# Seven block products in place of eight for one column chunk of gate and up, with a lag of four turns and nine pairs

## The chip, the cores and the metric

The kernel runs on one core of one Trainium2 chip. The metric is the time of one execution in microseconds of the device; several executions are timed and the median is given.

## The reference

The input is 256 tokens of 1024 float32 numbers. Four layers follow each other, and each has three blocks: a feed-forward block (FFN), a mixer, a second FFN. An FFN adds half of a SwiGLU to the tokens, with d_ff = 2816:

```
y = x * rsqrt(mean(x*x) + 1e-6) * g
x = x + 0.5 * ((silu(y @ w_gate) * (y @ w_up)) @ w_down)     # 1024 -> 2816 -> 1024
```

The mixers are, by layer: a gated short convolution, multi-head latent attention (MLA), a spatial gating MLP, and the convolution again. Each starts with the same norm and adds its result to x. All is float32.

## The kernel before

**Tiles and streams.** The 256 tokens are two tiles of 128 tokens. Each tile has a stream, a generator that walks through all twelve blocks (`stream`, `ffn`, `conv`, `mla`, `spatial`); each `yield` ends a turn. The loop at the end of `program` calls `advance` for tile 1 and then for tile 0 in each round, and tile 0 has had LAG = 3 turns ahead of that. So every engine gets its instructions in an order written out by hand, and all five engines run in that order. `later(n, fn)` puts a step off by n calls of `advance`.

**Products.** Each float32 operand is split in two parts, high and low, that TensorE takes in its fp32r format, and each product is three matmuls: high by high, high by low, low by high (`products`, L317, L318, L320). A weight unit is 1024 numbers per partition. `Weights` loads a unit into a raw buffer (N_RAW = 6), ScalarE makes the high part (L107), VectorE the low part (L113), as a pair of tiles in a pool of N_UNITS = 8 pairs. A unit is made AHEAD = 4 units before the leading tile needs it and is used by both tiles, by tile 1 three turns after tile 0. A turn of a tile in gate, up or down is one unit: six matmuls of 512 columns.

**An FFN.** The 2816 columns of gate and up are cut in FF_CHUNKS: five chunks of 512 columns and one of 256. For each chunk, eight k-tiles of 128 rows are accumulated in a bank of PSUM for gate (`gate_done` takes the bank through Silu on ScalarE, L475) and for up (`up_done` multiplies it by the gate on VectorE, L483, and turns 32 by 32 blocks over, L485). The first three of these run in a group (`linear_group`), then the rest one after the other (`linear`). The product is written to DRAM and read back transposed (`Turned`), split again by `take` (L308, L309) and multiplied by down (`rows_into_x`); there, the last DOWN_TAIL = 12 of the 22 k-tiles are done for the left half of the columns first and then for the right half.

**Between blocks.** `residual` adds each half of the result to x (L401, L403). `prepare_x` then squares it (L384), turns it over, by TensorE (`turn_by_pe`, L283, L444) or by VectorE and DRAM (L418, L424, L428, L434), multiplies by the gain and splits it (L275, L276) into `lhs[t][h]`. The norm's factor is applied later, with the evictions from PSUM. `normed` idles two turns of the stream, during which the other tile's matmuls run.

**Memory.** Most small tiles come from one pool of N_SLOTS = 34 slots of 2 KB per partition.

Of the kernel before, what the change touches and what calls it, by code (L numbers as in the profile page):

```python
# [40 lines left out]
N_UNITS = 8  # L41
N_RAW = 6
N_SLOTS = 34
# [4 lines left out]
LAG = 3  # L48
H_READ, H_TAKE = 7, 2
DOWN_TAIL, OUT_TAIL = 12, 4  # L50
# [86 lines left out]
@with_exitstack  # L137
def trunk(ctx: ExitStack, tc: tile.TileContext, x, positions, norm_g, ffn_gate, ffn_up, ffn_down,
          conv_w_in, conv_k, conv_w_out, mla_w_a, mla_q_norm, mla_w_uq, mla_kv_norm, mla_w_ukv,
          mla_q_gain, mla_k_gain, mla_w_o, sg_w_in, sg_v_norm, sg_w_s, sg_b, sg_w_out, out):  # L140
    const = ctx.enter_context(tc.tile_pool(name="const", bufs=1))
    raw_pool = ctx.enter_context(tc.tile_pool(name="raw", bufs=N_RAW))
    w_pool = ctx.enter_context(tc.tile_pool(name="w", bufs=N_UNITS))
# [5 lines left out]
    pools = const, raw_pool, w_pool, slots, bigs, small, dram, banks  # L149
    ins = (x, positions, norm_g, ffn_gate, ffn_up, ffn_down, conv_w_in, conv_k, conv_w_out, mla_w_a, mla_q_norm, mla_w_uq,  # L150
           mla_kv_norm, mla_w_ukv, mla_q_gain, mla_k_gain, mla_w_o, sg_w_in, sg_v_norm, sg_w_s, sg_b, sg_w_out, out)
    order = program(Blank(), [Blank()] * len(pools), None, *ins)
    with tc.manual_schedule(engines=MANUAL):
        program(tc.nc, pools, order, *ins)


def program(nc, pools, order, x, positions, norm_g, ffn_gate, ffn_up, ffn_down,
            conv_w_in, conv_k, conv_w_out, mla_w_a, mla_q_norm, mla_w_uq, mla_kv_norm, mla_w_ukv,
            mla_q_gain, mla_k_gain, mla_w_o, sg_w_in, sg_v_norm, sg_w_s, sg_b, sg_w_out, out):
    const, raw_pool, w_pool, slots, bigs, small, dram, banks = pools  # L160
# [32 lines left out]
    def run_due():  # L193
# [6 lines left out]
    W = Weights(nc, raw_pool, w_pool, {  # L200
        "gate": ffn_gate, "up": ffn_up, "down": ffn_down, "conv_in": conv_w_in, "conv_out": conv_w_out, "w_a": mla_w_a,
        "w_ukv": mla_w_ukv, "w_uq": mla_w_uq, "w_o": mla_w_o, "sg_in": sg_w_in, "sg_out": sg_w_out}, order)
    in_chain = [False] * NT
    pause = [0] * NT
    own = [0] * NT
# [12 lines left out]
    neg_half = fixed([P, 4], "neg_half")  # L218
    causal_r = fixed([P, P], "causal_r", F32R)
# [13 lines left out]
    def start():  # L233
        half = D // 2
        nc.sync.dma_start(out=xs[0][:, :half], in_=x[0, :P, :half])
        nc.scalar.dma_start(out=rows[0][: n_rows[0]], in_=norm_g.rearrange("i j (k p) -> (i j k) p", p=P))
        nc.sync.dma_start(out=xs[0][:, half:], in_=x[0, :P, half:])
# [5 lines left out]
        nc.gpsimd.memset(neg_half, -0.5)  # L243
        nc.vector.tensor_copy(out=ident_r, in_=ident)
# [24 lines left out]
        later(41, lambda: nc.vector.tensor_copy(out=causal_r, in_=causal))  # L269
# [21 lines left out]
    class Turned:  # L291
# [53 lines left out]
    def rows_into_x(t, a, m, n_kt, tail, factor, then):  # L345
# [33 lines left out]
    sums_of_x = [[None, None] for _ in range(NT)]  # L379

# [9 lines left out]
    def factor(sums):  # L390
        total = tiny(1, "total")
        nc.gpsimd.tensor_tensor(out=total, in0=sums[0], in1=sums[1], op=ALU.add)  # L392
        return power(total, EPS, 1.0 / D, 1, "rstd")
# [15 lines left out]
    def prepare_x(t, h, i, which, halves_by_dma):  # L409

        g = gain_at(i, which, h)
        lhs[t][h] = None
        later(1, lambda: square_x(t, h))
        if not halves_by_dma[h]:
            later(X_TURN, lambda: turn_by_pe(t, h, g))
            return
        z = slot([P, 4, 4, 32])
        nc.vector.transpose(z.rearrange("p j k b -> p k j b"), x_half(t, h).rearrange("p (k j b) -> p k j b", j=4, b=32))  # L418
# [12 lines left out]
        def take():  # L431
            xg = slot([P, 4, P])
            for k in range(4):
                nc.scalar.activation(xg[:, k, :].rearrange("p (i b) -> p i b", b=32), y[:, :, k], AF.Copy, scale=g[:, k : k + 1])  # L434
            lhs[t][h] = split(xg, [P, 4, P])

        later(X_WRITE, write)
        later(X_READ, read)
        later(X_TAKE, take)

    def turn_by_pe(t, h, g):
        tr = transposed([xs[t][:, (4 * h + k) * P : (4 * h + k + 1) * P] for k in range(4)])
        xg = slot([P, 4, P])
        nc.vector.tensor_tensor(out=xg, in0=tr, op=ALU.mult, in1=g.unsqueeze(2).broadcast_to([P, 4, P]))  # L444
        lhs[t][h] = split(xg, [P, 4, P])
# [11 lines left out]
    def normed(t, idle):  # L457
# [3 lines left out]
        return Lhs(t), factor(sums_of_x[t])  # L461


    def ffn(t, i, j, _, then):
        a, r = yield from normed(t, IDLE_FIRST if i + j == 0 else (IDLE_DMA, IDLE_PE)[j])
        gate, up, down = (("gate", i, j), ("up", i, j), ("down", i, j))
        hs = [None] * len(FF_CHUNKS)
        sg = [None] * len(FF_CHUNKS)
        z = []
        recs = []  # L470
# [6 lines left out]
        def up_done(n, ps):  # L477
            w = FF_CHUNKS[n][1]
            nk = sum(w for _, w in FF_CHUNKS[n - n % 2 : n - n % 2 + 2]) // P
            if n % 2 == 0:  # L480
                z[:] = [big([P, 4, nk, 32]), 0]
# [6 lines left out]
            if z[1] == nk:  # L488
                recs.append(Turned(z[0], nk))

        def body():
            yield from linear_group(t, a, [(gate, 0, lambda ps: gate_done(0, ps)), (up, 0, lambda ps: up_done(0, ps)),
                                           (gate, 512, lambda ps: gate_done(1, ps))], 512, NK)
            for n, (c, w) in enumerate(FF_CHUNKS):
# [3 lines left out]
                if n > 0:  # L498
                    up_done(n, (yield from linear(t, a, up, c, w, NK)))
                    yield  # L500
            yield from rows_into_x(t, lambda k: hs[k // 4], down, DFF // P, DOWN_TAIL, 0.5, then)

        def take(n):
            hs[n] = recs[n // 2].take(n % 2 * 4)

        events = {}
        for n in range(len(FF_CHUNKS)):
            k = 4 * n
            at = DFF // 64 + (k if k < DFF // P - DOWN_TAIL else DFF // P - DOWN_TAIL + (k - DFF // P + DOWN_TAIL) // 2)
            if n % 2 == 0:  # L510
                events.setdefault(at - H_READ, []).append(lambda n=n: recs[n // 2].read())
            events.setdefault(at - H_TAKE, []).append(lambda n=n: take(n))
        for at, _ in enumerate(body()):
            for event in events.get(at, ()):
                event()
            yield


    def conv(t, i, ia, shared, then):
# [49 lines left out]
        yield from rows_into_x(t, lambda k: ms[k // 4], ("conv_out", ia), NK, OUT_TAIL, 1.0, then)  # L569
# [27 lines left out]
    def spatial(t, i, ic, _, then):  # L597
# [3 lines left out]
        def v_done(v):  # L601
# [5 lines left out]
            if len(vs) == 2:  # L607
                rv.append(factor(sums))
# [41 lines left out]
        yield from rows_into_x(t, lambda k: ms[k // 4], ("sg_out", ic), NK, OUT_TAIL, 1.0, then)  # L650
# [129 lines left out]
    def mla(t, i, ib, shared, then):  # L780
# [174 lines left out]
        yield from rows_into_x(t, lambda k: os_[k // 4], ("w_o", ib), NK, OUT_TAIL, 1.0, then)  # L955
# [11 lines left out]
    def stream(t):  # L967
        for h in range(2):
            yield
            turn_by_pe(t, h, gain_at(0, 0, h))  # L970
            later(1, lambda h=h: square_x(t, h))
        for n, (kind, i, j) in enumerate(blocks):
# [17 lines left out]
    def advance(t):  # L990
# [3 lines left out]
        run_due()  # L994

# [35 lines left out]
```

## Time and profile before

| | |
|---|---|
| median of 3 runs | 1873.46 us (1873.39 to 1873.93) |
| the profiled execution's own time | 1871.69 us |
| its span, from the first to the last instruction | 1870.0 us |
| mean granted clock of TensorE, as a share of full speed | 0.996 |
| DMA, mean over the span | 214 GB/s |

Everything below is read from one profiled execution. Engines: PE is TensorE's matmuls, PEld its weight loads, DVE VectorE, ACT ScalarE, POOL GpSimd, SP the engine that issues most DMAs. Matmuls overlap in the array, so the time between the starts of two matmuls, and not the duration of one, tells how fast they go.

### The profile page before, as it was taken

What the parts mean: (1) busy time and instruction counts of PE and PEld (TensorE: products, weight loads), DVE (VectorE), ACT (ScalarE), POOL (GpSimd) and SP (SyncE); (2) the same over time, 40 slices, a digit from 0 to 9 for tenths busy, and PEclk for the clock granted to TensorE, in tenths of its full rate; (3) what the DMA queues carried; (4) which work ended last, traced back from release to release, by engine and by line L of the source; (5) the groups of instructions that cost most, each with busy time, mean ns of one, the idle gap of its engine ahead of it and who ended that gap; (6) DMA issues with size and microseconds to landing.
All of it is one profiled execution on the core that took longest, in us unless ns stands there. A gap on an engine that the chain in (4) does not pass through costs nothing.

```text
span 1870.0 us, 23382 instructions
## 1 busy us (share of the span) xinstructions
PE 1838.4 (98%) x8518; PEld 1508.3 (81%) x8518; DVE 1122.9 (60%) x1357; ACT 919.8 (49%) x1300; POOL 95.8 (5%) x222
## 2 busy tenths in 40 slices
PE   8999999999999989999999999999999999999999
PEld 6888877888888868788888888788888888778887
DVE  6556676555656576655565565655656565675563
ACT  5344545344544476544454456453445455545352
POOL 1000000000501031000010000000000000000000
PEclk9999999999999998999999999999999999999999
DMA  7678656678767740667876787566877686656683
GB/s 260 217 236 238 216 180 207 215 241 233 233 216 245 226 141 13 203 218 228 251 246 215 227 248 229 161 220 213 258 218 241 216 263 193 216 181 213 216 257 112
DMA packets 228981, 400.26 MB, mean 214 GB/s; under 512 B 17127, under 2 KB 77697, under 8 KB 228865
## 3 DMA queue, kind: packets, MB, share of 16 engines
q1 hardware_dynamic: 227856, 397.08, 67.5%
q8 instruction: 66, 1.08, 0.2%
q0 software_dynamic: 608, 1.11, 0.2%
q10 hardware_dynamic: 400, 0.57, 0.1%
q14 instruction: 51, 0.41, 0.1%
HBM read 365.67 MB, written 33.03 MB: 213 GB/s over the span
## 4 chain that ended last, share of the span: by engine, by line
PE 94%; DVE 3%; ACT 2%; issue 1%; DMA 0%; POOL 0%; DVEq 0%; ACTq 0%
PE acc L317 31%; PE acc L320 30%; PE acc L318 30%; PE tr L283 1%; DVE wlo L113 1%; PE acc L908 1%; PE acc L935 1%; DVE s L537 1%; ACT whi L107 0%; DVE x L401 0%; DVE s L535 0%; ACT s L833 0%; ACT s L275 0%; PE acc L624 0%; DMA s<-in_norm_g_dram 0%
## 5 line engine op out<-in xcount | busy, mean ns | idle before, releaser
L317 PE MATMUL acc<-whi,s 128*128 128x512 f32 (+1 forms) x2664 | 1025.3, 385 | 3.8 <-ACT s L275 2.9
L318 PE MATMUL acc<-wlo,s 128*128 128x512 f32 (+1 forms) x2664 | 1020.3, 383 | 1.5 <-DVE wlo L113 1.5
L320 PE MATMUL acc<-whi,s 128*128 128x512 f32 (+1 forms) x2664 | 989.1, 383 | 0.0
L113 DVE TENSOR_TENSOR wlo<-raw,whi 128x1024 fp32r<-128x1024 f32 (+1 forms) x634 | 749.0, 1212 | 282.7 <-ACT whi L107 277.9
L107 ACT ACTIVATE whi<-raw 128x1024 fp32r<-128x1024 f32 (+1 forms) x634 | 640.9, 1049 | 185.3 <-PE acc L320 155.8
L317 PEld LDWEIGHTS acc<-whi,s 128*128 128x128 f32 x2664 | 500.8, 188 | 108.7 <-ACT s L275 4.3
L320 PEld LDWEIGHTS acc<-whi,s 128*128 128x128 f32 x2664 | 500.9, 188 | 106.7 <-DVE s L276 1.0
L318 PEld LDWEIGHTS acc<-wlo,s 128*128 128x128 f32 x2664 | 501.1, 188 | 105.7 <-DVE wlo L113 2.3
L475 ACT ACTIVATE s<-acc,rstd 128x512 f32<-128x512 f32 (+1 forms) x96 | 62.6, 652 | 403.9 <-PE acc L320 403.9
L483 DVE SCALAR_TENSOR_TENSOR s<-acc,rstd,s 128x512 f32<-128x512 f32 (+1 forms) x96 | 67.8, 707 | 152.7 <-PE acc L320 152.7
L384 ACT ACTIVATE s<-x 128x512 bf16<-128x512 f32 x48 | 30.2, 630 | 160.3 <-DVE x L403 115.2
L309 DVE TENSOR_TENSOR s<-big,s 128x512 fp32r<-128x512 f32 x96 | 61.2, 638 | 50.4 <-ACT s L308 48.4
L392 POOL TENSOR_TENSOR total<-ss,ss 128x1 f32<-128x1 f32 x26 | 14.1, 544 | 1469.5 <-ACT s L384 1469.5
L403 DVE SCALAR_TENSOR_TENSOR x<-acc,x 128x512 f32<-128x512 f32 x32 | 22.1, 690 | 104.1 <-PE acc L320 104.1
L276 DVE TENSOR_TENSOR s<-s,s 128x512 fp32r<-128x512 f32 (+1 forms) x58 | 39.9, 688 | 73.1 <-ACT s L275 73.1
L485 DVE STREAM_TRANSPOSE big<-s 128x512 f32<-128x512 f32 (+1 forms) x96 | 64.1, 667 | 3.3
L308 ACT ACTIVATE s<-big 128x512 fp32r<-128x512 f32 x96 | 54.7, 582 | 16.5 <-DMA big<-turn 16.5
L275 ACT ACTIVATE s<-s 128x512 fp32r<-128x512 f32 (+1 forms) x58 | 36.5, 629 | 50.6 <-DVE s L544 28.6
L434 ACT ACTIVATE s<-s,columns 128x128 f32<-128x128 f32 x136 | 43.1, 388 | 24.0 <-DMA s<-xturn 24.0
L283 PE MATMUL tr<-ident,s 128*128 128x128 f32 (+1 forms) x222 | 34.2, 281 | 11.0 <-DVE s L778 6.6
L283 PEld LDWEIGHTS tr<-ident,s 128*128 128x128 f32 (+1 forms) x222 | 26.1, 139 | 19.6 <-DVE s L778 9.1
L418 DVE STREAM_TRANSPOSE s<-x 128x512 f32<-128x512 f32 x34 | 24.2, 712 | 1.2
(123 smaller groups left out, 407.3 us busy)
## 6 DMA issues: line engine op xcount, KB each, us to landing
raw<-in_ffn_gate_dram SPq DMA_DIRECT2D x176, 512.0 KB, 4.7
raw<-in_ffn_up_dram SPq DMA_DIRECT2D x176, 512.0 KB, 4.7
raw<-in_ffn_down_dram SPq DMA_DIRECT2D x176, 512.0 KB, 6.1
raw<-in_conv_w_in_dram SPq DMA_DIRECT2D x48, 512.0 KB, 4.7
turn<-big SPq DMA_DIRECT2D x32, 512.0 KB, 3.0
big<-turn SPq DMA_DIRECT2D x128, 128.0 KB, 5.2
xturn<-s SPq DMA_DIRECT2D x34, 256.0 KB, 4.3
s<-xturn SPq DMA_DIRECT2D x136, 64.0 KB, 2.0
```

The lines of the kernel that those rows point to most:

```text
L107: self.nc.scalar.activation(hi, self.loaded[u], AF.Copy)
L113: self.nc.vector.tensor_tensor(out=lo, in0=src, in1=hi.bitcast(F32), op=ALU.subtract)
L283: nc.tensor.transpose(tr[: part.shape[-1], n, :], part, ident)
L308: nc.scalar.activation(hi.rearrange("p k (i b) -> p k i b", b=32), src, AF.Copy)
L309: nc.vector.tensor_tensor(out=lo.rearrange("p k (i b) -> p k i b", b=32), in0=src, in1=hi.bitcast(F32).rearrange("p k (i b) -> p k i b", b ...
L317: nc.tensor.matmul(ps, lhsT=ah[:, k, :], rhs=wh[:, wk, c], start=first, stop=False)
L318: nc.tensor.matmul(ps, lhsT=ah[:, k, :], rhs=wl[:, wk, c], start=False, stop=False)
L320: nc.tensor.matmul(ps, lhsT=al[:, k, :], rhs=wh[:, wk, c], start=False, stop=last)
L434: nc.scalar.activation(xg[:, k, :].rearrange("p (i b) -> p i b", b=32), y[:, :, k], AF.Copy, scale=g[:, k : k + 1])
L475: nc.scalar.activation(sg[n], ps[:, :w], AF.Silu, scale=r)
L483: nc.vector.scalar_tensor_tensor(out=h, in0=ps[:, :w], scalar=r, in1=sg[n], op0=ALU.mult, op1=ALU.mult)
L485: nc.vector.transpose(z[0][:, :, k0 : k0 + w // P].rearrange("p j k b -> p k j b"), h.rearrange("p (k j b) -> p k j b", j=4, b=32))
```

## The change

In seven of the eight FFNs (all but the first) chunk 4 of gate and up, columns 2048 to 2560, is no longer computed by each stream for itself. A third generator, `sevens`, called the lane below, computes it for both tiles together. The 256 x 1024 left side is seen as 2 x 2 blocks of 128 x 512, the 1024 x 512 right side as 2 x 2 blocks of 512 x 256, and the product is made from seven block products in place of eight. A block product is four k-tiles of three matmuls with 256 columns. Sums of the blocks of both sides are formed on VectorE and then split in high and low as before; weight blocks are loaded by DMAs of their own into five buffers (`sevens_pool`), and their pairs come from the pool of weight pairs. Banks are read out in between (`snapshot`, `add`), and the last steps (`gate_halves`, `up_halves`) make the gated product and turn it over.

The lane is advanced by `beside` after each `advance`, 0.6 of a step per call, from the moment when all four halves of the left side are there. It has six steps ahead of the products, two per product, and up to four behind.

So that sums over both tiles have rows of like size, x is scaled before it is turned over wherever an FFN follows (`even`, on ScalarE, with the factor of the block just done), and the turning over by TensorE comes one call later. The FFN's factor is multiplied by the inverse of that one on GpSimd.

The lag is four turns. When tile 0 has had ten turns of an FFN, `follow(1)` makes it pause three rounds, so that the lag is one; when the lane ends, `follow(4)` makes tile 1 pause three rounds. The pool of pairs has nine; there are five raw buffers and 27 slots. Down takes chunk 4 last, and its tail is 10.

```diff
-N_UNITS = 8
-N_RAW = 6
-N_SLOTS = 34
+N_UNITS = 9
+N_RAW = 5
+N_SEVENS_RAW = 5
+N_SLOTS = 27
-LAG = 3
+LAG = 4
+CLOSE_AT, CLOSE_LAG = 10, 1
+SEVENS, RATE = (4,), 0.6
+SEVENS_TAIL = 10
...
-    def prepare_x(t, h, i, which, halves_by_dma):
+    def prepare_x(t, h, i, which, halves_by_dma, evened):
...
+        def even():
+            src[0] = slot([P, 512])
+            nc.scalar.activation(src[0], x_half(t, h), AF.Copy, scale=scales[t][0])
...
+        if evened:
+            even()
+        if halves_by_dma[h]:
+            later(evened, lambda: turn_half(src[0], take, X_TAKE - evened))
+        else:
+            later(X_TURN + evened, lambda: turn_by_pe(t, h, g, src[0]))
...
+        if t == NT - 1 and seven:
+            lanes.append(sevens(i, j, seven, shared))
...
+        if seven and t == 0:
+            events.setdefault(CLOSE_AT, []).append(lambda: follow(CLOSE_LAG))
...
+    def follow(turns):
+        t = int(turns > lag[0])
+        pause[t] += abs(turns - lag[0])
+        lag[0] = turns
...
+    def sevens(i, j, chunks, shared):
...
+        for block in ("11", "12", "22", "21"):
+            load(0, block)
...
+        def combine(x, y, op):
+            f = slot([P, 4, P])
+            nc.vector.tensor_tensor(out=f, in0=x, in1=y, op=op)
+            return f
...
+            nc.scalar.activation(hi, src, AF.Copy)
+            forms[key] = hi, lo, src
+
+        def low(key):
+            hi, lo, src = forms[key]
+            nc.vector.tensor_tensor(out=lo, in0=src, in1=hi.bitcast(F32), op=ALU.subtract)
...
+        left = (a11, forms["s1"], forms["s2"], a12, forms["s3"], a22, forms["s4"])
+        right = ("11", "11", "11", "21", "12", "11", "22")
+        added = (None, "12", "22", None, "22", "21", None)
+        last = 7 * len(units) - 1
+
+        def sum_of(s):
+            u, q = divmod(s, 7)
+            if s <= last and added[q]:
+                to = raws[u][right[q]]
+                nc.vector.tensor_tensor(out=to, in0=to, in1=raws[u][added[q]], op=ALU.add)
...
+        for s in range(last + 1):
+            u, q = divmod(s, 7)
+            if s + 1 <= last:
+                low(s + 1)
+            sum_of(s + 2)
...
+            if pending:
+                pending.pop(0)()
+            if q == 1:
+                v1 = snapshot(y)
+            elif q == 3:
+                v2 = snapshot(y)
+            elif q == 4:
+                vs = [slot([P, 512]) for _ in range(NT)]
+                add(vs[0][:, :256], x, v1, ALU.add)
+            elif q == 5:
+                v3 = snapshot(y)
+            elif q == 6:
+                add(vs[1][:, 256:], z, v3, ALU.subtract)
+            yield
...
+            ps = (y, z, y, x, y, y, z)[q]
+            ah, al, wh, wl = left[q][0], left[q][1], forms[s][0], forms[s][1]
+            for k in range(4):
+                for n, (f, w) in enumerate(((ah, wh), (ah, wl), (al, wh))):
+                    nc.tensor.matmul(ps[:, :256], lhsT=f[:, k, :], rhs=w[:, k, :], start=q in (0, 1, 3) and k + n == 0, stop=k == 3 and n == 2,
+                                     skip_group_check=True)
+            del forms[s]
+            high_of(s + 2)
...
+            yield
...
+        follow(LAG)
...
+    def beside():
+        credit[0] += RATE
+        while lanes and credit[0] >= 1 and all(half_ is not None for tile_ in lhs for half_ in tile_):
+            credit[0] -= 1
+            if next(lanes[0], "end") == "end":
+                lanes.pop()
+                credit[0] = 0.0
```

## Rows read from the trace of the kernel before

**Rows 1.** The page: busy time, share of the span and instructions by engine.
```profile
PE 1838.4 (98%) x8518; PEld 1508.3 (81%) x8518; DVE 1122.9 (60%) x1357; ACT 919.8 (49%) x1300; POOL 95.8 (5%) x222
```

**Rows 2.** The chain that ended last, shares of the span by engine.
```profile
PE 94%; DVE 3%; ACT 2%; issue 1%; DMA 0%; POOL 0%; DVEq 0%; ACTq 0%
```

**Rows 3.** Waits of PE: for whom, total us, times, longest.
```profile
PE tr L283 <- DVE x L401: 7.4, 4, 1.9
PE tr L283 <- DVE s L778: 6.6, 7, 1.5
PE acc L317 <- ACT s L275: 2.9, 2, 2.2
...
PE acc L318 <- DVE wlo L113: 1.5, 2, 0.8
```

**Rows 4.** PE in order of time, 512 columns: start, duration; 27 in the stretch.
```profile
479.77 0.39 PE L320 MATMUL acc<-whi,s 128*128 128x512 f32 x1
...
485.82 0.39 PE L318 MATMUL acc<-wlo,s 128*128 128x512 f32 x1
```

**Rows 5.** The same, twelve matmuls of 256 columns between others of 512, twice.
```profile
402.37 0.28 PE L317 MATMUL acc<-whi,s 128*128 128x256 f32 x1
...
403.80 0.40 PE L317 MATMUL acc<-whi,s 128*128 128x512 f32 x1
...
415.08 0.28 PE L317 MATMUL acc<-whi,s 128*128 128x256 f32 x1
...
416.49 0.39 PE L317 MATMUL acc<-whi,s 128*128 128x512 f32 x1
```

**Rows 6.** Busy time by engine in ten us, nearly all matmuls of 256 columns.
```profile
410.00:420.00 10.00, 10.00 (x73) 9.33 (x72) 6.92 (x9) 5.82 (x8) 0.00 (x0) 1.00 0.80 278
```

**Rows 7.** The page's costliest groups: the weight loads of one line, mean ns.
```profile
L317 PEld LDWEIGHTS acc<-whi,s 128*128 128x128 f32 x2664 | 500.8, 188 | 108.7 <-ACT s L275 4.3
```

**Rows 8.** Groups by form: us busy, mean ns of one, idle before them.
```profile
L113 DVE TENSOR_TENSOR wlo<-raw,whi 128x1024 fp32r<-128x1024 f32 x626 | 741.5, 1215 | 281.6 <-ACT whi L107 276.8 <-DMA raw<-in_ffn_up_dram 2.0 <-DMA raw<-in_mla_w_a_dram 1.0
L276 DVE TENSOR_TENSOR s<-s,s 128x512 fp32r<-128x512 f32 x56 | 38.8, 692 | 71.9 <-ACT s L275 71.9
L483 DVE SCALAR_TENSOR_TENSOR s<-acc,rstd,s 128x512 f32<-128x512 f32 x80 | 60.1, 751 | 134.7 <-PE acc L320 134.7
L485 DVE STREAM_TRANSPOSE big<-s 128x512 f32<-128x512 f32 x80 | 56.9, 712 | 2.8
L483 DVE SCALAR_TENSOR_TENSOR s<-acc,rstd,s 128x256 f32<-128x256 f32 x16 | 7.8, 485 | 18.0 <-PE acc L320 18.0
L309 DVE TENSOR_TENSOR s<-big,s 128x256 fp32r<-128x256 f32 x16 | 6.7, 421 | 13.9 <-ACT s L308 13.9
L107 ACT ACTIVATE whi<-raw 128x1024 fp32r<-128x1024 f32 x626 | 634.4, 1051 | 185.3 <-PE acc L320 155.8 <-DVE s L309 8.8 <-issue 5.0
L275 ACT ACTIVATE s<-s 128x512 fp32r<-128x512 f32 x56 | 35.4, 632 | 47.7 <-DVE s L544 28.6 <-DVE s L444 18.1
L308 ACT ACTIVATE s<-big 128x256 fp32r<-128x256 f32 x16 | 6.4, 401 | 0.0
```

**Rows 9.** One gate and up stretch, 296 to 412 us: busy, PE, PEld, DVE, ACT.
```profile
sum 116.00, PE 116.00 PEld 95.19 DVE 65.87 ACT 53.87 POOL 0.93; mean PE 9.67 PEld 7.93 DVE 5.49 ACT 4.49 POOL 0.08
```

**Rows 10.** What DVE waited for in that stretch.
```profile
L113 DVE TENSOR_TENSOR wlo<-raw,whi 128x1024 fp32r<-128x1024 f32 x42 | 49.3, 1212 | 29.7 <-ACT whi L107 29.7
L483 DVE SCALAR_TENSOR_TENSOR s<-acc,rstd,s 128x512 f32<-128x512 f32 x10 | 7.5, 751 | 17.8 <-PE acc L320 17.8
```

**Rows 11.** In order of time where tile 1 passes from a mixer to an FFN.
```profile
288.76 1.18 DVE L113 TENSOR_TENSOR wlo<-raw,whi 128x1024 fp32r<-128x1024 f32 x1
...
289.87 0.68 DVE L401 TENSOR_TENSOR x<-acc,x 128x512 f32<-128x512 f32 x1
...
290.60 0.66 PE L283 MATMUL tr<-ident,x 128*128 128x128 f32 x4 [1.84 <-DVE x L401]
```

**Rows 12.** Start of down in one FFN, 413 to 470 us: its sum, and ACT's waits.
```profile
sum 57.00, PE 57.00 PEld 46.73 DVE 35.99 ACT 30.06 POOL 0.00; mean PE 57.00 PEld 46.73 DVE 35.99 ACT 30.06 POOL 0.00
...
L107 ACT ACTIVATE whi<-raw 128x1024 fp32r<-128x1024 f32 x21 | 21.8, 1055 | 14.5 <-PE acc L320 12.3 <-issue 1.3 <-ACT s L308 0.9
...
L308 ACT ACTIVATE s<-big 128x512 fp32r<-128x512 f32 x9 | 5.5, 618 | 0.9 <-DMA big<-turn 0.9
```

**Rows 13.** The MLA's first part, 660 to 715 us: busy by engine.
```profile
660.00:715.00 55.00, 41.73 (x233) 34.32 (x232) 40.20 (x115) 45.36 (x99) 21.64 (x31) 0.97 0.34 112
```

More of the change, by code (lines that the diff above doesn't have):

```diff
@@ L198, in run_due @@
             p[2]()
-    W = Weights(nc, raw_pool, w_pool, {
+    matrices = {
         "gate": ffn_gate, "up": ffn_up, "down": ffn_down, "conv_in": conv_w_in, "conv_out": conv_w_out, "w_a": mla_w_a,
-        "w_ukv": mla_w_ukv, "w_uq": mla_w_uq, "w_o": mla_w_o, "sg_in": sg_w_in, "sg_out": sg_w_out}, order)
+        "w_ukv": mla_w_ukv, "w_uq": mla_w_uq, "w_o": mla_w_o, "sg_in": sg_w_in, "sg_out": sg_w_out}
+    W = Weights(nc, raw_pool, w_pool, matrices, order)
     in_chain = [False] * NT
     pause = [0] * NT
+    lag = [LAG]
+    lanes = []
+    credit = [0.0]
     own = [0] * NT
@@ L218, in program @@
     neg_half = fixed([P, 4], "neg_half")
+    half = fixed([P, 1], "half")
     causal_r = fixed([P, P], "causal_r", F32R)
@@ L243, in start @@
         nc.gpsimd.memset(neg_half, -0.5)
+        nc.gpsimd.memset(half, 0.5)
         nc.vector.tensor_copy(out=ident_r, in_=ident)
@@ L390, in factor @@
     def factor(sums):
-        total = tiny(1, "total")
+        total, m = tiny(1, "total"), tiny(1, "ms")
         nc.gpsimd.tensor_tensor(out=total, in0=sums[0], in1=sums[1], op=ALU.add)
-        return power(total, EPS, 1.0 / D, 1, "rstd")
+        nc.gpsimd.tensor_scalar(m, total, 1.0 / D, EPS, op0=ALU.mult, op1=ALU.add)
+        r, rms = tiny(1, "rstd", 8), tiny(1, "rms", 8)
+        nc.gpsimd.tensor_tensor(out=r, in0=m, in1=neg_half[:, :1], op=ALU.pow)
+        nc.gpsimd.tensor_tensor(out=rms, in0=m, in1=half, op=ALU.pow)
+        return r, rms
     def x_half(t, h):
@@ L429, in read, with turn_by_pe @@
             W.hold(-1)
[L431 to L435, printed above, removed]
         later(X_WRITE, write)
         later(X_READ, read)
-        later(X_TAKE, take)
-    def turn_by_pe(t, h, g):
-        tr = transposed([xs[t][:, (4 * h + k) * P : (4 * h + k + 1) * P] for k in range(4)])
+        later(turns, lambda: take(y))
+    def turn_by_pe(t, h, g, src):
+        tr = transposed([src[:, k * P : (k + 1) * P] for k in range(4)])
         xg = slot([P, 4, P])
         nc.vector.tensor_tensor(out=xg, in0=tr, op=ALU.mult, in1=g.unsqueeze(2).broadcast_to([P, 4, P]))
-        lhs[t][h] = split(xg, [P, 4, P])
+        lhs[t][h] = split(xg, [P, 4, P]) + (xg,)
     class Lhs:
@@ L460, in normed, with ffn @@
         in_chain[t] = False
-        return Lhs(t), factor(sums_of_x[t])
-    def ffn(t, i, j, _, then):
-        a, r = yield from normed(t, IDLE_FIRST if i + j == 0 else (IDLE_DMA, IDLE_PE)[j])
+        r, rms = factor(sums_of_x[t])
+        last, scales[t] = scales[t], (r, rms)
+        if evened:
+            r = tiny(1, "evened", 8)
+            nc.gpsimd.tensor_tensor(out=r, in0=scales[t][0], in1=last[1], op=ALU.mult)
+        return Lhs(t), r
+    def ffn(t, i, j, shared, then):
+        with_sevens = i + j > 0
+        seven = SEVENS if with_sevens else ()
+        a, r = yield from normed(t, IDLE_FIRST if i + j == 0 else (IDLE_DMA, IDLE_PE)[j], with_sevens)
+        shared["r", t] = r
+        if t == NT - 1 and seven:
+            lanes.append(sevens(i, j, seven, shared))
         gate, up, down = (("gate", i, j), ("up", i, j), ("down", i, j))
+        plain = [n for n in range(len(FF_CHUNKS)) if n not in seven]
+        ks = [k for n in plain + list(seven) for k in range(4 * n, 4 * n + FF_CHUNKS[n][1] // P)]
+        tail = SEVENS_TAIL if seven else DOWN_TAIL
+        full = len(ks) - tail
         hs = [None] * len(FF_CHUNKS)
@@ L478, in up_done @@
             w = FF_CHUNKS[n][1]
-            nk = sum(w for _, w in FF_CHUNKS[n - n % 2 : n - n % 2 + 2]) // P
-            if n % 2 == 0:
-                z[:] = [big([P, 4, nk, 32]), 0]
+            at = plain.index(n)
+            if at % 2 == 0:
+                nk = sum(FF_CHUNKS[m][1] for m in plain[at : at + 2]) // P
+                z[:] = [(big if nk > 4 else slot)([P, 4, nk, 32]), 0, []]
             h = slot([P, w])
@@ L487, in up_done @@
             z[1] += w // P
-            if z[1] == nk:
-                recs.append(Turned(z[0], nk))
+            z[2].append((n, k0))
+            if at % 2 == 1 or at == len(plain) - 1:
+                rec = Turned(z[0], z[1])
+                for m, k0 in z[2]:
+                    shared["rec", t, m] = rec, k0
         def body():
@@ L493, in body @@
                                            (gate, 512, lambda ps: gate_done(1, ps))], 512, NK)
-            for n, (c, w) in enumerate(FF_CHUNKS):
+            for n in plain[1:]:
+                c, w = FF_CHUNKS[n]
                 if n > 1:
@@ L497, in body, with read @@
                     yield
[L498 to L501, printed above, removed]
+                up_done(n, (yield from linear(t, a, up, c, w, NK)))
+                yield
+            yield from rows_into_x(t, lambda k: hs[k // 4], down, ks, tail, 0.5, then)
+        def read(n):
+            rec, k0 = shared["rec", t, n]
+            if k0 == 0:
+                rec.read()
         def take(n):
-            hs[n] = recs[n // 2].take(n % 2 * 4)
+            rec, k0 = shared["rec", t, n]
+            hs[n] = rec.take(k0)
         events = {}
+        first = sum(FF_CHUNKS[n][1] for n in plain) // 64
         for n in range(len(FF_CHUNKS)):
[L508 to L511, printed above, removed]
+            k = ks.index(4 * n)
+            at = first + (k if k < full else full + (k - full) // 2)
+            events.setdefault(at - H_READ, []).append(lambda n=n: read(n))
             events.setdefault(at - H_TAKE, []).append(lambda n=n: take(n))
+        if seven and t == 0:
+            events.setdefault(CLOSE_AT, []).append(lambda: follow(CLOSE_LAG))
         for at, _ in enumerate(body()):
@@ L568, in conv @@
             yield
-        yield from rows_into_x(t, lambda k: ms[k // 4], ("conv_out", ia), NK, OUT_TAIL, 1.0, then)
+        yield from rows_into_x(t, lambda k: ms[k // 4], ("conv_out", ia), range(NK), OUT_TAIL, 1.0, then)
     sg_wT = [fixed([P, 4, P], f"sg_wT{j}") for j in range(2)]
@@ L607, in v_done @@
             if len(vs) == 2:
-                rv.append(factor(sums))
+                rv.append(factor(sums)[0])
                 for j in range(2):
@@ L649, in spatial @@
         yield
-        yield from rows_into_x(t, lambda k: ms[k // 4], ("sg_out", ic), NK, OUT_TAIL, 1.0, then)
+        yield from rows_into_x(t, lambda k: ms[k // 4], ("sg_out", ic), range(NK), OUT_TAIL, 1.0, then)
     qk_gain = fixed([P, 1], "qk_gain")
@@ L954, in mla @@
             yield
-        yield from rows_into_x(t, lambda k: os_[k // 4], ("w_o", ib), NK, OUT_TAIL, 1.0, then)
+        yield from rows_into_x(t, lambda k: os_[k // 4], ("w_o", ib), range(NK), OUT_TAIL, 1.0, then)
     kinds = {"ffn": (ffn, None), "conv": (conv, None), "mla": (mla, prepare_mla), "spatial": (spatial, prepare_spatial)}
@@ L994, in advance @@
         run_due()
+        if lanes:
+            beside()
+    def beside():
[5 more added lines that the diff above has]
+                credit[0] = 0.0
     for _ in range(LAG):
```

149 lines of the change are left out of this document (127 added, 22 removed).

## The prediction

> **What bounds the kernel now.** I read the busy times first: PE has work in 98% of the span, DVE in 60%, ACT in 49% [rows 1]. A busy share alone doesn't say who waits for whom, so the chain of waits comes next: 94% of what ended last is PE [rows 2]. Then PE's own waits: the longest entries are a few us each, and all of them together some 27 us, at the start, in the MLA and where a tile passes to an FFN [rows 3]. Inside an FFN PE doesn't wait: 116.0 us busy of 116, with DVE at 65.9 and ACT at 53.9 [rows 9]. So time is bought by giving PE fewer columns, if the other engines can keep up with what is made in their place.
>
> **What the change takes from PE.** From the start at 479.77 to that at 485.82 there are 26 steps, 232.7 ns for 512 columns [rows 4]. Twelve matmuls of 256 columns between others take 1.43 us at 402.37 and 1.41 us at 415.08 [rows 5]; I take 1.42. One chunk of gate or up costs two tiles x 8 k-tiles x 3 = 48 matmuls of 512, 11.17 us. Seven block products of twelve cost 7 x 1.42 = 9.94 us. That is 1.23 us a matrix; seven FFNs x 2 matrices are 14: **17.2 us**. Half of 232.7 is 116.4 ns, so 256 columns cost 118 in place of 116, and only 0.2 us a matrix is lost to that. Down and the transposes stay as they were.
>
> PEld is busy 9.33 of 10 us among matmuls of 256 columns [rows 6], so the weight load needs a look. One load lasts 188 ns [rows 7], longer than the 118 ns from one such matmul to the next, so loads overlap other work here. If they could not, a matmul of 256 would take 188 ns at least: 84 x 0.188 = 15.8 us a matrix against 11.2, +65 us in all, 1938 us. The Trainium skill ("TensorE: Matmul & The Clock Gate", The mechanism, in Part 3) says that a weight load overlaps running matmuls only where the row groups differ; with its figure for a load (128 columns at 1.2 GHz, 107 ns, section LDWEIGHTS) added to each matmul, 84 x 0.214 against 48 x 0.320 would be an estimate of +37 us. The trace's 118 ns doesn't agree with that rule, so I give this case 1 in 100.
>
> **What it adds to DVE and ACT.** Per matrix seven weight forms replace four units: 3 more highs (1.051 us each) and lows (1.215) [rows 8]. Four sums of weight blocks of 1024 columns are new; the trace has no such add, and I take the 1.215 of the subtraction of the same shape (between 0.69 for half the columns and twice that, 1.38). Per FFN come four sums of left blocks and four splits, at 0.69 on DVE and 0.63 on ACT. Evictions: before, 2 x (0.751 + 0.712) = 2.9 us of DVE for both matrices; after, six adds of 256 columns at 0.42, two products at 0.485, one at 0.751, two transposes at 0.712, 5.7 us. DVE: 42 x 1.215 + 56 x 1.215 + 56 x 0.69 + 7 x 2.8 = 177 us more, 1300 of about 1857: 70%. ACT: 42 x 1.05 + 28 x 0.63, plus 28 scalings of x at 0.63 and 42 snapshots at 0.40, is 96 us more: 55%.
>
> The share over the span hides the stretch that counts. A product of the lane takes two steps at 0.6 a call: 3.33 calls. PE per product: 3.33 x 6 x 0.2327 + 1.42 = 6.07 us. DVE: 1.67 unit lows (2.03), one form low (1.22), 4/7 of a sum (0.69), the plain evictions (2.93 per 16 calls: 0.61), the lane's (5.7/14 = 0.40): 4.95 us, 82%. ACT by the same count some 57%. Cost taken: nothing, hidden by PE's 6.07, because a unit is made four ahead and a form's low is issued a step and a half, about 7 us, ahead of its product. Without that cover each us over 6.07 costs 98 us (7 x 14 products).
>
> **Where a wait is short.** In each unit two evictions come just one step ahead of a matmul that writes the same bank. ACT's third snapshot must end before product 5: it has one or two calls, 1.4 to 2.8 us, and needs some 0.7. Before product 6 DVE must do the next form's low, a sum and the add: 1.05 (the high on ACT) + 1.22 + 1.22 + 0.42 and some 0.2 of signals = 4.1 us after product 5, if no buffer is free sooner. PE has 4.66 us of tile work between them. One unit's high and low in front adds 2.27 and makes a stall of 1.7. All tile matmuls stand behind the waiting one. Bounds: 0 to 1.7 us x 14 = 24; I take 0.2 x 14 = 3, since the pool mostly has another pair free and the chain starts earlier.
>
> **Closing and opening the lag.** Tile 0's pause costs PE nothing: tile 1 uses pairs that are made. When tile 1 pauses, tile 0 needs three units in three turns of 1.40 us, against 1.22 on DVE and 1.05 on ACT for each, plus `take` (0.69 and 0.62). Four made pairs and five raw buffers stand in reserve. At the start of down ACT already waits for PE (12.3 us) and once for a read back from DRAM (0.9), so there is slack, but reads and `take` now have three turns of half the length [rows 12]. Bounds 0 to 2 us x 7; taken 0.3, 2 us. The five smaller loads and one raw buffer less are covered as long as ACT waits for PE and not for a DMA.
>
> **Between blocks.** Where an FFN follows, `even` puts 0.63 us of ACT between `residual` and the transpose, and the transpose comes one call later, behind one more unit of tile 1 (1.40 us). In the trace tile 1's transposes waited 1.84 us for the residual, which had itself waited for a low of 1.18 [rows 11]; four such waits make 7.4 [rows 3]. New: 288.76 + 1.18 + 0.69 + 0.63 + 0.1 = 291.4 against PE free at about 290.2: 1.2 us. With a unit's high in front of `even`, 2.3. Bounds 4 x (-1.8 to +0.5); taken -1 in all. Elsewhere the lag of four covers one more turn. In the MLA's first part PE is busy 41.7 of 55 us with ACT at 45.4 [rows 13]; there it can win or lose a few us, -4 to +4, taken 0. The start has one more turn of tile 0 alone: -1 to +1.5, taken 0.
>
> **The sum.** 1871.7 (profiled execution) - 17.2 + 3 + 2 - 1 = 1858.5. The median of the runs lies 1.8 above that execution: **1860 us**. Its own range: gain 17.2 less 0 to 9 lost, and 5 either way for MLA and start: 1851 to 1868.
>
> **The rivals.** A: product 6 waits for DVE each time, 1 us x 14 on top of my 3: 1872 to 1874, no change. For it: the chain of 4.1 us against 4.66. Against: the pool's other free pairs. B: the openings cost 1.5 us each and ACT's head waits for DMA: 1860 + 8 = 1868. For it: the one wait for a read [rows 12]; against: nine units of reserve. C, slower: DVE becomes the bound beside the lane. Place: the 98 products. A low waited 29.7 us / 42 = 0.71 us for its high in the old stretch [rows 10]. If 0.60 of that stays with each of 2.67 lows a product, DVE needs 4.95 + 1.60 = 6.55, 0.48 over PE, x 98 = 47: 1902 us. It decides from 0.49 us a low: 6.07 + 17.2/98 = 6.25 against 4.95 + 1.30. Against it: PE waited for nothing in that stretch, so these were waits of an engine that was ahead. D: 256 columns go no better in the lane than 133 ns (84 x 0.133 = 11.17), so nothing is saved, 1873 and up; the two mixed stretches speak against it, the rule on loads is its extreme.
>
> **Chances.** Forecast 0.60, A 0.15, B 0.12, C 0.09, D 0.04 (the loads' 0.01 in it). 0.2% is 3.7 us and about what a measurement of this kernel can tell from no change: faster is below 1869.7, slower above 1877.2. Faster: 0.60 + 0.11 of B + 0.05 of A = 0.76. Slower: C 0.09 + 0.03 of A + 0.02 of D = 0.14. The rest, 0.10, is the same. The range leaves out C and the ends of A: 1850 to 1876.
>
> **What would show it.** Right: 672 fewer matmuls of 512 and 1176 more of 256, spaced 118 ns; PE's waits in an FFN still near nothing; DVE near 80% and not full beside the lane. Waits of PE for the third add or snapshot would show A; for a `take` or a low in the three turns after the lane, B; PE waiting for lows of forms, with DVE full, C. The prediction is wrong if PE's waits grow by over 10 us, whatever line they name.

## Result: 3.9% slower, and where the time went

The changed kernel takes 1945.56 us (median of 4 runs, 1942.21 to 1950.66) against 1873.56 before: ratio 1.0386, 95% interval 1.0363 to 1.0409. The forecast was 1860 with a range up to 1876, so it missed in sign. The profiled execution took 1946.05 us by itself, with a span of 1944.3 and a mean granted clock of 0.978 (before 0.996).

The page first, engines by busy time, share and instructions, to be held against [rows 1]:

```profile
span 1944.3 us, 24911 instructions
PE 1854.1 (95%) x9022; PEld 1535.9 (79%) x9022; DVE 1280.7 (66%) x1560; ACT 1009.3 (52%) x1447; POOL 131.9 (7%) x263
...
PE 46%; DVE 5%; DMA 5%; ACT 4%; issue 2%; SPq 1%; ACTq 0%; DVEq 0%
```

The last line is the chain that ended last [rows 2]: PE's share falls from 94% to 46%. PE is idle 1944.3 - 1854.1 = 90.2 us, before it was 31.6. That is 58.6 us more. And PE is *busier* than before, 1854.1 against 1838.4, with fewer columns to stream. The clock tells why: a mean of 0.978 means 2 x 0.022 x 1944 = 85 us at the lower of the two levels (1.2 GHz in place of 2.4), before 2 x 0.004 x 1870 = 15. PE was idle for a part of that time. In the eight longest stretches at the lower clock, the start of each lane among them, it was busy for 53.4 of 78.2 us (the first of the eight, and the sum; behind the length stands PE's busy time):

```profile
322.00:332.20 10.20, 7.56 (x23) 6.18 (x24) 9.24 (x10) 5.47 (x6) 0.00 (x0) 0.50 0.38 108
...
sum 78.20, PE 53.39 PEld 43.67 DVE 68.22 ACT 41.70 POOL 10.51; mean PE 6.67 PEld 5.46 DVE 8.53 ACT 5.21 POOL 1.31
```

With the shorter stretches some 61 us of matmuls ran at the lower clock, and in the kernel before 13. Half of the 47 us more, some 24, is lost. The sum 58.6 + 24 - 17.2 (the saved matmuls of the forecast) = 65; for the other 9 of the 74.4 us by which the two profiled executions differ there is no term.

PE's waits say where [rows 3]: for whom, total us, times, longest.

```profile
PE acc L328 <- DVE wlo L117: 42.0, 12, 6.5
PE acc L327 <- ACT s L285: 19.5, 15, 4.4
PE acc L744 <- DVE wlo L613: 7.7, 7, 1.1
PE tr L293 <- DVE s L1019: 5.9, 6, 2.2
```

Unit lows (L117) cost 42.0 us where it had been 1.5, and the longest single wait is 6.5. L744 is the lane's matmul, and it waits 7 times: once a lane, for the first product. The split left halves (L285) cost 19.5 where it had been 2.9.

Here is one of these holes, with some lines of its stretch (start, duration, in brackets the idle time before and whom it waited for):

```profile
311.58 1.06 ACT L111 ACTIVATE whi<-raw 128x1024 fp32r<-128x1024 f32 x1 [2.62 <-DMA raw<-in_ffn_gate_dram]
...
313.11 1.27 ACT L441 ACTIVATE s<-s,columns 128x128 f32<-128x128 f32 x4
...
315.07 0.69 DVE L286 TENSOR_TENSOR s<-s,s 128x512 fp32r<-128x512 f32 x1 [4.29 <-ACT s L285]
...
315.68 0.69 DVE L603 TENSOR_TENSOR s<-s,s 128x512 f32<-128x512 f32 x1
...
316.40 0.63 ACT L608 ACTIVATE s<-s 128x512 fp32r<-128x512 f32 x1 [1.36 <-DVE s L603]
...
317.07 0.69 DVE L613 TENSOR_TENSOR s<-s,s 128x512 fp32r<-128x512 f32 x1 [0.70 <-ACT s L608]
317.68 0.68 DVE L603 TENSOR_TENSOR s<-s,s 128x512 f32<-128x512 f32 x1
...
319.67 0.68 DVE L603 TENSOR_TENSOR s<-s,s 128x512 f32<-128x512 f32 x1
...
321.66 0.68 DVE L603 TENSOR_TENSOR s<-s,s 128x512 f32<-128x512 f32 x1
322.27 1.22 DVE L117 TENSOR_TENSOR wlo<-raw,whi 128x1024 fp32r<-128x1024 f32 x1
...
323.54 0.79 PE L328 MATMUL acc<-wlo,s 128*128 128x512 f32 x1 [4.50 <-DVE wlo L117]
```

Read it from the end. PE waits 4.50 us for the low of a unit, made at 322.27. That unit's high was issued at 311.58, so its low was possible from 312.6. VectorE stood still then: next in its order came the split of tile 1's last left half (L286), which waited 4.29 us for ScalarE. When that was done, at 315.68, the lane was free to start. The section on the change says that the lane is advanced from the moment when all four halves are there; its credit, though, counts from the moment when the lane is made. In the code (`beside`) it had grown for eight calls, to 8 x 0.6 = 4.8, so four steps came in a single call: sum on VectorE (L603, four times), high on ScalarE (L608), low on VectorE (L613), each waiting for the one before, 2 us a round. Only behind all this, in program order, stands the unit's low. From 312.6 to 322.3 VectorE made no unit low, while PE used up the units that had been made ahead.

What follows shows in the windows (PE, PEld, DVE, ACT, POOL busy, granted clock, DMA share, GB/s):

```profile
319.00:323.50 4.50, 0.04 (x1) 0.00 (x0) 3.74 (x6) 1.78 (x4) 0.00 (x0) 0.84 0.73 232
323.50:331.00 7.50, 6.36 (x20) 5.27 (x21) 6.58 (x7) 3.75 (x5) 0.00 (x0) 0.50 0.50 141
331.00:338.00 7.00, 7.00 (x35) 5.89 (x35) 6.93 (x8) 4.41 (x6) 0.00 (x0) 0.91 0.47 142
```

PE does nothing for 4.5 us, then runs 7.5 us at half clock (20 matmuls, among them the wait of 1.1 for the first product), and gets its clock back in the third stretch. The clock was lower already at the end of the hole (a mean of 0.84). All seven lanes begin like this, with holes of 4.5 to 6.5 us.

After the beginning the lane does what was forecast. From 335 to 405 us PE waits for nothing:

```profile
335.00:405.00 70.00, 70.00 (x374) 59.94 (x373) 51.76 (x53) 37.90 (x47) 0.00 (x0) 1.00 0.61 192
```

and one product, from its first matmul to the next tile matmul, takes 1.42 us, the number of the forecast:

```profile
353.32 0.28 PE L744 MATMUL acc<-whi,s 128*128 128x256 f32 x1
...
354.74 0.39 PE L327 MATMUL acc<-whi,s 128*128 128x512 f32 x1
```

### The profile page after: what moved, and what is told of

Same layout as the page of the kernel before. It is cut to its first block, busy times and chain, and to the rows that moved or that the text cites. A ratio compares the mean times of both kernels' runs of the same rounds, so it can differ in the third digit from the quotient of the medians.

```text
span 1944.3 us, 24911 instructions
## 1 busy us (share of the span) xinstructions
PE 1854.1 (95%) x9022; PEld 1535.9 (79%) x9022; DVE 1280.7 (66%) x1560; ACT 1009.3 (52%) x1447; POOL 131.9 (7%) x263
## 4 chain that ended last, share of the span: by engine, by line
PE 46%; DVE 5%; DMA 5%; ACT 4%; issue 2%; SPq 1%; ACTq 0%; DVEq 0%
PE acc L327 13%; PE acc L328 13%; PE acc L330 13%; PE acc L744 5%; DMA xturn<-s 2%; DVE wlo L117 2%; ACT whi L111 1%; DMA raw<-in_ffn_gate_dram 1%; PE tr L293 1%; ACT s L441 1%; SPq L465 1%; DVE s L603 1%; ACT s L608 1%; PE acc L1176 1%; PE acc L1149 1%
## 5 line engine op out<-in xcount | busy, mean ns | idle before, releaser
L328 PE MATMUL acc<-wlo,s 128*128 128x512 f32 (+2 forms) x2440 | 939.2, 385 | 42.0 <-DVE wlo L117 42.0
L327 PE MATMUL acc<-whi,s 128*128 128x512 f32 (+2 forms) x2440 | 944.2, 387 | 22.6 <-ACT s L285 19.5
L330 PE MATMUL acc<-whi,s 128*128 128x512 f32 (+2 forms) x2440 | 903.3, 385 | 0.0
L117 DVE TENSOR_TENSOR wlo<-raw,whi 128x1024 fp32r<-128x1024 f32 (+1 forms) x578 | 686.3, 1212 | 159.5 <-ACT whi L111 157.3
L111 ACT ACTIVATE whi<-raw 128x1024 fp32r<-128x1024 f32 (+1 forms) x578 | 588.8, 1048 | 193.0 <-DMA raw<-in_ffn_down_dram 103.5
L327 PEld LDWEIGHTS acc<-whi,s 128*128 128x128 f32 x2440 | 462.5, 190 | 119.0 <-ACT s L285 26.3
L330 PEld LDWEIGHTS acc<-whi,s 128*128 128x128 f32 x2440 | 462.6, 190 | 102.7 <-DVE s L286 6.4
L744 PE MATMUL acc<-whi,s 128*128 128x256 f32 x784 | 162.7, 290 | 0.0
L608 ACT ACTIVATE whi<-block 128x1024 fp32r<-128x1024 f32 x98 | 103.4, 1055 | 111.3 <-DVE block L640 111.3
L744 PEld LDWEIGHTS acc<-whi,s 128*128 128x128 f32 x784 | 134.0, 198 | 4.7
L613 DVE TENSOR_TENSOR wlo<-block,whi 128x1024 fp32r<-128x1024 f32 x98 | 118.7, 1212 | 23.1 <-ACT whi L608 22.7
L744 PE MATMUL acc<-wlo,s 128*128 128x256 f32 x392 | 115.0, 293 | 7.7 <-DVE wlo L613 7.7
L286 DVE TENSOR_TENSOR s<-s,s 128x512 fp32r<-128x512 f32 (+1 forms) x58 | 39.8, 687 | 97.5 <-ACT s L285 97.5
L744 PEld LDWEIGHTS acc<-wlo,s 128*128 128x128 f32 x392 | 77.4, 197 | 15.3 <-DVE wlo L613 11.3
L640 DVE TENSOR_TENSOR block<-block,block 128x1024 f32<-128x1024 f32 x56 | 68.4, 1221 | 1.0
L436 ACT ACTIVATE s<-x,rstd 128x512 f32<-128x512 f32 x28 | 20.3, 724 | 81.4 <-DVE x L420 47.7
```

The lines of the kernel that those rows point to most:

```text
L111: self.nc.scalar.activation(hi, self.loaded[u], AF.Copy)
L117: self.nc.vector.tensor_tensor(out=lo, in0=src, in1=hi.bitcast(F32), op=ALU.subtract)
L327: nc.tensor.matmul(ps, lhsT=ah[:, k, :], rhs=wh[:, wk, c], start=first, stop=False)
L328: nc.tensor.matmul(ps, lhsT=ah[:, k, :], rhs=wl[:, wk, c], start=False, stop=False)
L330: nc.tensor.matmul(ps, lhsT=al[:, k, :], rhs=wh[:, wk, c], start=False, stop=last)
L608: nc.scalar.activation(hi, src, AF.Copy)
```

## Experiments

Theory 1: the lane's first steps, in a burst, stand on VectorE and ScalarE ahead of unit lows and starve PE; the rest is the clock that falls behind the hole. Theory 2: the weights land late (one raw buffer less, four block loads more). Theory 3: VectorE is overloaded beside the lane. Ratios are to the kernel before, run on the same chip (its own median there 1871.4 to 1873.6). PE's idle time is span less busy time.

| | us | ratio (95%) | PE idle | clock |
|---|---|---|---|---|
| before | 1873.56 | 1 | 31.6 | 0.996 |
| the change | 1945.56 | 1.0386 (1.0363 to 1.0409) | 90.2 | 0.978 |
| E1 no burst | 1906.70 | 1.0190 (1.0156 to 1.0224) | 61.1 | 0.990 |
| E2 unit lows ahead of the burst | 1956.72 | 1.0450 (1.0416 to 1.0484) | 107.0 | 0.975 |
| E3 six raw buffers | 1927.23 | 1.0299 (1.0273 to 1.0325) | 71.8 | 0.978 |
| E4 no lane | 1875.78 | 1.0021 (1.0007 to 1.0035) | 31.4 | 0.996 |
| E5 only the lane's first steps | 1931.85 | 1.0328 (1.0309 to 1.0347) | 70.5 | 0.984 |
| E6 no burst, six raw | 1877.82 | 1.0037 (1.0024 to 1.0051) | 47.1 | 0.996 |
| E7 no burst, first steps in order | 1875.60 | 1.0027 (1.0014 to 1.0041) | 42.4 | 0.996 |
| E8 as E7, six raw, tail 12 | 1848.44 | 0.9881 (0.9863 to 0.9900) | 24.8 | 0.996 |
| E9 the change, first steps in order | 1919.57 | 1.0261 (1.0240 to 1.0283) | 66.9 | 0.986 |
| E10 as E7, tail 12 | 1865.72 | 0.9969 (0.9957 to 0.9981) | 32.9 | 0.995 |
| E11 as E7, six raw | 1863.13 | 0.9957 (0.9941 to 0.9974) | 33.6 | 0.997 |

**E1, no burst.**

```diff
     def beside():
+        if not all(half_ is not None for tile_ in lhs for half_ in tile_):
+            return
         credit[0] += RATE
```

> The lane's credit grows only once all four halves of the left side are there, so its first steps come one at a time and not three or four in one call. Theory 1 (the burst of left sums and splits stands on DVE and ACT ahead of the next unit's low, and TensorE starves): the holes of 5 to 6.5 us at the start of each of the seven lanes shrink to under 1.5 us and the clock stays up there; 1870 to 1895 us. Theory 2 (the raw units land late, since one raw buffer is gone and four block loads compete): the holes stay, 1935 to 1946 us. Theory 3 (DVE is too busy beside the lane as a whole): the waits move to the products, over 1920 us.

39 us come back, less than theory 1 said. PE's waits for unit lows fall from 42.0 to 2.1, so the burst did make those. But the waits for the lane's first products grow from 7.7 to 21.7 us, fourteen of them, two a lane:

```profile
PE acc L327 <- ACT s L285: 17.7, 15, 5.0
PE acc L744 <- DVE wlo L613: 11.8, 7, 1.8
PE acc L744 <- ACT whi L608: 9.9, 7, 2.0
...
PE acc L328 <- DVE wlo L117: 2.1, 3, 0.8
```

Theory 3 does not hold: these are first products, not products along the lane.

**E2, unit lows ahead of the burst.**

```diff
         if lanes:
+            W.complete()
             beside()
```

> The same burst, but the lows of units whose highs are issued stand ahead of it. Theory 1: one of the two lows that TensorE misses comes 6 us earlier, the next is still behind the burst; holes about half as long, 1900 to 1925 us. Theory 2: no change, 1940 to 1950 us.

A miss: 11 us slower than the change, and both theories had said otherwise. The unit lows are on time (2.1 us), and the same first product pays for it:

```profile
PE acc L744 <- ACT whi L608: 44.7, 7, 6.8
...
PE acc L744 <- DVE wlo L613: 19.4, 7, 2.8
...
PE acc L328 <- DVE wlo L117: 2.1, 3, 0.8
```

PE runs in program order, so whichever of the two it meets first holds up everything. The first product's matmuls stand a fixed number of calls behind the burst. Moving the lows changes which of them is late, not that VectorE and ScalarE have too much to do between the moment when the last half is there and the first product. Why the two waits together became longer than before was not followed up.

**E3, six raw buffers** (N_RAW 6, and 25 slots to make room).

> Six raw buffers as in the kernel before, two slots fewer (25) to make room. Theory 2: holes under 2 us, 1885 to 1905 us. Theory 1: holes as they were, 1935 to 1950 us.

Between the two: 18 us come back, so theory 2 has a share (or the slots, which change with it). ScalarE's waits for raw units show it, for the change first:

```profile
ACT whi L111 <- DMA raw<-in_ffn_down_dram: 103.5, 79, 3.1
...
ACT whi L111 <- DMA raw<-in_ffn_gate_dram: 27.7, 8, 5.3
```

and with six buffers:

```profile
ACT whi L111 <- DMA raw<-in_ffn_down_dram: 38.3, 39, 1.9
...
ACT whi L111 <- DMA raw<-in_ffn_gate_dram: 1.0, 1, 1.0
```

The gate units are the first of an FFN: ScalarE waited 2.62 us for one at 311.58 above, and the last left half stood behind it in its order. Holes remain (32.3 us for unit lows in 10 waits), with the clock at 0.978.

**E4, no lane** (SEVENS = ()). With the lane two things fall away that the code makes depend on it: down's tail is 12 again, and the lag isn't closed to one and opened again.

> No chunk goes to the lane: all chunks by the streams, with the lag of four, nine pairs, five raw buffers, 27 slots and the scaled x of the changed kernel. Theory 1: no holes in the FFNs; the time is that of the kernel before plus what scaling x costs between blocks, 1872 to 1885 us. If the lag, the pools or the scaling make the holes: over 1900 us.

As theory 1 expects: 1875.78 us. The lag of four, nine pairs, five raw buffers, fewer slots and the scaling of x together cost 0.2% (the interval reaches from 0.07% to 0.35%). So these don't make the loss; it needs the lane, or the tail and the lag that come with it. Five raw buffers do no such harm without it, although ScalarE waits 35.8 us for gate units here too.

**E5, only the lane's first steps.** The generator ends after the four left sums and their splits; no blocks are loaded, nothing is multiplied, and all chunks come from the streams.

```diff
...
+        if not chunks:
+            return
         left = (a11, forms["s1"], forms["s2"], a12, forms["s3"], a22, forms["s4"])
```

> All chunks are made by the streams as without the lane, but the lane's first four steps (the four left sums and their splits) still run, in a burst and without use; no weight blocks, no products. Theory 1 (the burst itself starves TensorE of unit lows): holes of 4 to 6 us at seven places, with the clock falling behind them; 1905 to 1930 us against 1876 without any lane. Theory 2 (block loads and late raw units): within 5 us of 1876. Theory 4 (the wait is for the first product, which stands too soon behind the preamble): also near 1876, since no product waits.

This is the disputed cost by itself: 56 us over E4 (1931.85 against 1875.78) for work that VectorE and ScalarE do in 1152.8 - 1117.2 = 36 and 951.6 - 935.0 = 17 us of busy time, all of it off PE. That is 2 us above what theory 1 expected. The tail and the lag are as in E4, so they are not needed for the holes. Theory 1 is shown, theory 4 (only the first product waits) is out, and block loads are not needed either. The matmuls of E4 and E5 are the same, so the two also give the price of a hole: PE is idle for 70.5 - 31.4 = 39.1 us more, and its busy time is 1858.4 - 1843.1 = 15.3 us longer, at a mean clock of 0.984 in place of 0.996.

```profile
PE acc L328 <- DVE wlo L117: 44.3, 12, 6.5
PE acc L327 <- ACT s L285: 8.6, 8, 2.6
```

The first line is close to that of the change (42.0, 12, 6.5).

**E6, no burst and six raw buffers.**

> No burst, and six raw buffers with 25 slots. If late raw units are a second cause beside the burst: TensorE's 22 us of waits for the first products fall to under 10, 1880 to 1892 us. If the rest is the back and forth of DVE and ACT alone: as without the burst, 1900 to 1910 us.

Waits for the first products fall to 11.4 us (10.1 in 7 for lows, 1.3 in 2 for highs), a little over the ten expected; the time, 1877.82 us, is 2 us under its expected interval. The raw units (and two slots fewer, which go with the sixth buffer) were a second cause, worth 29 us by medians here.

**E7, first steps in order, no burst, five raw buffers.** The same sums, highs and lows, each one step behind what it needs:

```diff
         s1 = combine(a21[2], a22[2], ALU.subtract)
+        s3 = combine(a11[2], a21[2], ALU.subtract)
+        yield
         high("s1", s1, None, [P, 4, P])
+        s2 = combine(s1, a11[2], ALU.subtract)
+        high("s3", s3, None, [P, 4, P])
         yield
         low("s1")
-        s2 = combine(s1, a11[2], ALU.subtract)
         high("s2", s2, None, [P, 4, P])
+        s4 = combine(a12[2], s2, ALU.add)
+        low("s3")
...
```

> No burst, and the six steps in front of the products are laid out so that ScalarE's high of a sum is issued a step after VectorE's sum, and the low a step after that; same work, five raw buffers. If the back and forth between DVE and ACT delays the first product: its waits (22 us without the burst) fall to under 10, 1880 to 1892 us. If the raw units set it: no change, 1900 to 1910 us.

31 us less than E1. The lane's first products wait 2.6 us in all, and with the short waits gone the clock is back at 0.996. The time is 4 us under the expected interval. So the 22 us in E1 had both causes: E6's cure takes half of these waits away, E7's most, and either brings some 30 us back.

**E8, all of it** (E7 with six raw buffers, 25 slots and SEVENS_TAIL = 12).

> No burst, the six steps laid out in order, six raw buffers with 25 slots, and down's tail 12 as in the kernel before. If these four are what the lane loses: waits back to 30 to 35 us in all, and the 17 us of saved matmuls show, 1858 to 1868 us, faster than the kernel before. If something else in the lane costs (products, evictions): 1875 us or more.

1848.44 us, 1.2% under the kernel before and 10 us under the low end of what was expected. PE's page line and waits:

```profile
PE 1823.0 (99%) x9022; PEld 1521.5 (82%) x9022; DVE 1274.2 (69%) x1560; ACT 1003.7 (54%) x1447; POOL 143.5 (8%) x263
...
PE tr L293 <- DVE s L1019: 5.6, 7, 2.2
PE acc L328 <- DVE wlo L117: 3.6, 6, 0.8
PE acc L327 <- ACT whi L111: 2.6, 2, 1.3
...
PE acc L327 <- ACT s L285: 1.3, 1, 1.3
```

PE is busy 1838.4 - 1823.0 = 15.4 us less than before, with a clock that is the same: that is near the saving of the forecast (17.2), less some 2. It is idle 24.8 us in place of 31.6, since the waits of a mixer's transposes for the residual (7.4 us before) are not among its waits any more.

**E9, first steps in order, but still in a burst.**

> The changed kernel with only the six steps in front of the products laid out one engine after the other; the first three or four still come in one call. If the burst does harm because DVE waits for ACT four times in a row: that is nearly gone, 1890 to 1905 us. If it does harm by where it stands, a block of work ahead of the units' lows: DVE still has 5 us of it there, 1915 to 1940 us.

1919.57 us: 26 less than the change, so the back and forth was a part; but 44 more than E7, so most of the harm is that a block of work stands there at all. PE still waits 23.8 us for unit lows.

**E10 and E11, E7 with one of the other two.**

> The kernel without the burst and with the steps laid out (1876 us), with down's tail at 12. If the shorter tail is what makes the next FFN's first matmul wait for its split left half (16.5 us in 14 waits there): those waits fall under 5, 1858 to 1864 us. If the raw buffers are the cause: 1870 us or more.

> The same kernel (1876 us) with six raw buffers and 25 slots, tail 10. It should give what is left of the way to 1848 us: 1860 to 1866 us, with the waits for the split left half still there, some 10 us.

Tail 12 takes 10 us off E7, six raw buffers 12, and both together 27. With tail 12 alone the waits for the split left half fall from 16.5 to 7.7, with six raw buffers alone to 11.1, with both to 1.3. E10's waits stayed over the 5 us expected and its time 2 us over its interval; both causes are in those waits. They are at the passage from one FFN to the next layer's. In the changed kernel:

```profile
480.71 0.68 DVE L420 SCALAR_TENSOR_TENSOR x<-acc,x 128x512 f32<-128x512 f32 x1
481.43 0.72 ACT L436 ACTIVATE s<-x,rstd 128x512 f32<-128x512 f32 x1 [0.95 <-DVE x L420]
...
482.67 1.27 ACT L441 ACTIVATE s<-s,columns 128x128 f32<-128x128 f32 x4
...
484.65 0.50 PE L327 MATMUL acc<-whi,s 128*128 128x512 f32 x1 [1.22 <-ACT s L285]
```

The first half's take (L441) is due a fixed number of calls after its residual. With a tail one turn shorter per half it comes behind the second half's residual in ScalarE's order (the scaling L436 waits for it), and PE waits for what the take makes. With a tail of 12 (E10) it comes first, at 465.89 against 469.73, and PE doesn't wait there:

```profile
465.89 1.27 ACT L441 ACTIVATE s<-s,columns 128x128 f32<-128x128 f32 x4
...
469.73 0.72 ACT L436 ACTIVATE s<-x,rstd 128x512 f32<-128x512 f32 x1 [0.95 <-DVE x L420]
```

## Why the prediction was wrong

**Right.** What bounds the kernel; the size of the saving (1.42 us a product as measured, 672 and 1176 matmuls); that products, snapshots and adds along the lane cost nothing: the term of 3 us "where a wait is short" was 0 between 335 and 405 us, and in the whole trace PE waits at L744 only for the seven first products, so rival A fell. VectorE beside the lane was 51.8 of 70 us, 74% where 82% was worked out, and ScalarE 54%: rival C, the one with the right sign, fell too. Opening the lag left no wait of PE that shows (rival B), and rival D is out by the 1.42.

**The step that failed** is the cost put on VectorE and ScalarE: "Cost taken: nothing, hidden by PE's 6.07, because a unit is made four ahead". That is an average over the 98 products, and along the lane it held. The six steps ahead of the products were counted into the totals (56 x 0.69) but never given a place. Four of them come at once, since the credit runs on while the lane waits; they wait for one another across two engines, 2 us a round; and in VectorE's order they stand between the high and the low of a unit that PE needs. The cover of units made ahead was no help there: in the hole shown it had been drawn on already by a raw unit that landed late and by the wait for the last left half. E5 measures the four left sums and their splits alone, 56 us where I had 0. Of the 97 us between the change and E8, 70 went with the burst and the order of the first steps (E7), the other 27 with the raw buffers, the slots and the tail. The prediction's own sign of being wrong appeared: PE's waits grew by over 10 us, from 27 to 85.

**The second part of the miss** is that a stall was priced by its length. 58.6 us more of idle time came with some 24 lost at the lower clock, most of them behind the holes; E6 with 47.1 us idle in waits of at most 2.2 kept 0.996.

**"The five smaller loads and one raw buffer less are covered"** failed in part: ScalarE waited 154.8 us for raw units (103.5, 27.7, 15.8, 6.5, 1.3) where it had been 8.3, and E3 (18 us) and E11 (12 us) show what it cost, each with 25 slots. **"Between blocks ... taken -1"** looked at the transposes after a mixer, and those did get better. It left out what the shorter tail does at the passage between two FFNs: the waits for the split left half went from 2.9 to 19.5 us, and E10 gets 10 us back.

**Two slips in the working**, on which the miss doesn't hang. The upper end of the range 1851 to 1868 comes to 1870 by its own terms (1873.5 - 17.2 + 9 + 5). And a form's low is issued three steps of the lane ahead of its product, not a step and a half; the 7 us beside it fit the three steps.

What stays open: the share of the 25 slots, which no run tells apart from the sixth raw buffer; the 9 us without a term in the sum of the result; and why the low-clock stretch behind a hole lasts as long as it does.

## What to carry to other kernels

When work moves to engines that have room on average, find where in each engine's order its *first* instructions land, and what stands behind them; here 36 us of VectorE's work, harmless by its amount, stood in a block ahead of what PE needed and cost 56 (E5). Work that is paced by a credit must not save the credit up while it can't run. And lay out a chain across two engines so that each link is issued one step behind the link that it needs.

## What the hardware showed

After 4.5 us without a matmul the granted clock was 0.50 for the next 7.5 us, and in the next 7 us its mean was 0.91. At 0.50 matmuls of 512 columns started 0.42 to 0.43 us apart, against 0.233 before:

```profile
324.56 0.63 PE L327 MATMUL acc<-whi,s 128*128 128x512 f32 x1
324.98 0.63 PE L328 MATMUL acc<-wlo,s 128*128 128x512 f32 x1
```

A hole so cost some 1.4 times its length: in E5 against E4, with the same matmuls, 39.1 us more of idle time and 15.3 of slower matmuls.
